# Two of the four weight sums of each Strassen unit made by transfers that add into SBUF

## The chip, the cores and the metric

The kernel runs on one core of one Trainium2 chip, as one program. The metric is device time in microseconds (us): the median of several runs. The engines are TensorE (PE in the profile, with its weight loads as PEld), VectorE (DVE), ScalarE (ACT), GpSimd (POOL) and SyncE (SP, which here only issues transfers). Each engine has one queue of its own that it works off in order; transfers are issued from an engine's queue and then carried out by the core's 16 DMA engines.

## The reference

The reference is one decoder layer on 512 tokens of width 1024 in float32: a half-step SwiGLU feed-forward network (FFN), a token mixer (a gated recurrence beside attention), and a second half-step FFN. The change touches only the last product of both FFNs, the one with `w_down`:

```
def _swiglu(x, w_gate, w_up, w_down):
    return (jax.nn.silu(x @ w_gate) * (x @ w_up)) @ w_down
...
x = x + 0.5 * _swiglu(_rms_norm(x, ffn1_norm[l]), ffn1_w_gate[l], ffn1_w_up[l], ffn1_w_down[l])
```

Here `w_gate` and `w_up` are 1024 x 2816, and `w_down` is 2816 x 1024.

## The kernel before

Everything is kept transposed: features lie on the 128 partitions, tokens along the free dimension. Float32 products are made from two parts each, a high part (a copy rounded to the format that PE multiplies fast, made by ACT at L127) and a low part (what is left, made by DVE at L129); a product is three matmuls, high by high, high by low and low by high. `parts` makes the two parts of a weight tile; `weights` loads a tile and calls it. The tiles of the high and low parts have four buffers each.

An FFN (`ffn`) treats the 2816 hidden features as 22 blocks of 128, in chunks of 6, 6, 6 and 4. `products(f)` makes the gate and up products of a block, and `hidden` scales them and combines them on DVE and ACT. For the first three chunks the down projection goes by Strassen's scheme in Winograd's form, which does a 2 x 2 block product with seven block products in place of eight. The blocks on the weights' side are pairs of hidden blocks against two output blocks of 128 (output block k and k + 4); on the other side are the two halves of 256 tokens. `operands` prepares the seven combinations of hidden blocks for a pair of hidden blocks.

One unit is `down(k, ...)`: output blocks k and k + 4 of one chunk, m = 3 pairs of hidden blocks, so w = 384 columns per weight block. It does four things:

- L319 and L320: SP loads the raw tile (tag "wd", two buffers), 128 x 4 x 384, 768 KB: the four weight blocks of the unit side by side.
- L321 to L327: DVE makes four sums of these blocks in the sums tile (tag "ws", two buffers): one instruction of 768 columns makes sums 1 and 2 (L323), and two of 384 columns make sum 0 (L326) and sum 3 (L327). The first of them is queued behind an instruction of `hidden` by `issue_after`.
- L329: the seven weight operands (raw blocks and sums) form four groups: raw 0 and 1; sums 0 and 1; sums 2 and 3; raw 3. `parts` makes the high and low parts of a group when its first product is traced (L337).
- L354 to L368: seven products (steps) of 9 matmuls, each followed by a DVE instruction at L350 that adds the partial result into `x`. Groups one to three serve two steps each, the fourth one step.

Units run in pairs, k = 0 and 1, then 2 and 3, and the loop at L381 interleaves the two units of a pair: two steps of the one, two of the other, and so on. There are 2 FFNs x 3 chunks x 4 units = 24 units, so 12 pairs; a stretch of down products (two pairs, 252 matmuls) stands between the `products` of one chunk and the next, six stretches in all. In the profile the tiles of the first FFN end in "a", those of the second in "b": `rda` and `rdb` are the raw tiles, `sda` and `sdb` the sums, `h_da` and `l_da` the high and low parts of a group, `pda` and `pdb` the PSUM results.

The last chunk of four blocks is done without the scheme (`down_plain`).

The program is written with a framework that draws the order of every engine's queue at build time, by simulating the whole program (`schedule_with_timeline_sim=True`, L951), subject to the program's data dependences, the buffers of each tag, and the explicit `issue_after` blocks. A changed instruction can therefore move others. Tiles that are opened later in the same SBUF space wait for the earlier ones to be released.

POOL works in three places: it adds up the squares for the norms (L167), takes the power for the reciprocal root (L186), and does parts of the mixer. It issues no transfer in the kernel before; all transfers are SP's.

On the host `_layout` brings the weights into the order in which they are loaded: `by_pairs` puts, for each chunk, the blocks of output block k and of k + 4 next to each other, and within each the even hidden blocks ahead of the odd ones.

Of the kernel before, what the change touches and what calls it, by code (L numbers as in the profile page):

```python
# [8 lines left out]
F32 = mybir.dt.float32  # L9
# [3 lines left out]
ALU = mybir.AluOpType  # L13
PSUM = bass.MemoryType.PSUM

P = 128
T = 512
D = 1024
KD = D // P
DFF = 2816  # L20
NF = DFF // P
# [28 lines left out]
def hybrid_layer_kernel(  # L50
# [17 lines left out]
    nc = tc.nc  # L68
# [18 lines left out]
    def f32(ap):  # L87
        return ap.bitcast(F32)

    def bank(name, tag="b"):  # L90
        return banks["pool"].tile([P, T], F32, tag=tag, name=name, bufs=banks["tags"][tag])
# [28 lines left out]
    def weights(src, name, n=KD * P, rows=1):  # L120
        raw = wpool.tile([P, n], F32, tag="wr", name=f"r_{name}")
        nc.sync.dma_start(raw if rows == 1 else raw.rearrange("p (k m) -> p k m", k=rows), src)
        return parts(raw, name, n)

    def parts(raw, name, n):
        hi = wpool.tile([P, n], F32R, tag="wh", name=f"h_{name}", bufs=4)
        nc.scalar.copy(hi, raw)  # L127
        lo = wpool.tile([P, n], F32R, tag="wl", name=f"l_{name}", bufs=4)
        nc.vector.tensor_sub(lo, raw, f32(hi))  # L129
        return hi, lo  # L130

    def weights_early(*args):
# [79 lines left out]
    def ffn(name, xn, wg, wu, wd, first, done):  # L212
# [20 lines left out]
        with tc.tile_pool(name=f"ffn_{name}", bufs=2, reuse_waits="tile") as fp:  # L233
# [81 lines left out]
            def down(k, col, m, bs, after):  # L315

                n = f"{name}{col}_{k}"
                w = m * P
                raw = fp.tile([P, 4, w], F32, tag="wd", name=f"rd{n}")  # L319
                nc.sync.dma_start(raw, wd[k, :, 4 * col * P : 4 * col * P + 4 * w])  # L320
                sums = fp.tile([P, 4, w], F32, tag="ws", name=f"sd{n}")  # L321
                with tc.issue_after(after.ins):
                    nc.vector.tensor_add(  # L323
                        sums[:, 1:3, :], raw[:, 2:3, :].to_broadcast([P, 2, w]), raw[:, 0:4:3, :][:, ::-1, :]
                    )
                nc.vector.tensor_add(sums[:, 0, :], raw[:, 0, :], sums[:, 1, :])  # L326
                nc.vector.tensor_add(sums[:, 3, :], raw[:, 1, :], sums[:, 0, :])  # L327
                flat = "p s w -> p (s w)"
                srcs = (raw[:, 0:2, :], sums[:, 0:2, :], sums[:, 2:4, :], raw[:, 3:4, :])  # L329
                ws = []  # L330
                banks_ = [bank(f"pd{n}_{c}", "y")[:, :TH] for c in range(2)]
                lo_, hi_ = x[k], x[k + KD // 2]

                def product(pt, group, half, b, start):
                    if group == len(ws):
                        src = srcs[group]
                        ws.append(parts(src.rearrange(flat), f"d{n}_{group}", src.shape[1] * w))  # L337
                    wh, wl = ws[group]
                    for i in range(m):
                        s = slice((half * m + i) * P, (half * m + i + 1) * P)  # L340
                        bh, bl = bs[i][0][:, b, :], bs[i][1][:, b, :]
                        for q, (p, a) in enumerate(((wh, bh), (wh, bl), (wl, bh))):
                            nc.tensor.matmul(  # L343
                                pt, p[:, s], a, start=start and i == 0 and q == 0,
                                stop=i == m - 1 and q == 2, skip_group_check=True,
                            )

                def collect(pt, xk, half, by):
                    t = slice(half * TH, (half + 1) * TH)
                    nc.vector.scalar_tensor_tensor(  # L350
                        xk[:, t], pt, by, xk[:, t], op0=ALU.mult, op1=ALU.add
                    )

                u, v = banks_  # L354
                steps = [
                    [(u, 0, 0, B11, True), (lo_, 0, 0.5)],
                    [(v, 0, 1, B21, True), (lo_, 0, 0.5)],
                    [(u, 1, 0, T2, False), (lo_, 1, 0.5)],
                    [(v, 1, 1, T1, True), (hi_, 1, -0.5)],
                    [(u, 2, 0, T3, False), (hi_, 1, -0.5)],  # L360
                    [(v, 2, 1, B22, False), (lo_, 1, 0.5)],
                    [(u, 3, 0, T4, False), (hi_, 0, -0.5)],
                ]
                for p, c in steps:
                    def step(p=p, c=c):
                        product(*p)
                        collect(p[0], *c)
                    yield step  # L368

            f0 = 0  # L370
            for nf in CHUNKS[:-1]:
                bs, after = [], None
                for i in range(nf // 2):
                    bs.append(operands(f0 + 2 * i, i))

                    after = hidden.last if i == nf // 2 - 2 else after
                f0 += nf
                ahead.append(products(f0))
                for k in range(0, KD // 2, 2):
                    two = [list(down(k + i, (f0 - nf) // 2, nf // 2, bs, after)) for i in range(2)]  # L380
                    for r in (slice(0, 2), slice(2, 4), slice(4, 6), slice(6, 7)):  # L381
                        for steps in two:
                            for step in steps[r]:
                                step()
# [332 lines left out]
    with tc.tile_pool(name="att", bufs=2, reuse_waits="tile") as ap:  # L717
# [108 lines left out]
        for j, pair in enumerate(pairs):  # L826
            ws = []
# [43 lines left out]
def _layout(x, ffn1_norm, ffn1_w_gate, ffn1_w_up, ffn1_w_down, mix_norm, w_in,  # L871
            conv_w, conv_b, rg_w_a, rg_b_a, rg_w_x, rg_b_x, rg_lambda,
            q_norm, k_norm, rnn_out_norm, attn_out_norm, w_out,
            ffn2_norm, ffn2_w_gate, ffn2_w_up, ffn2_w_down):
    import numpy as np

    def cols(v):
        return np.asarray(v).reshape(-1, P).T

    def by_block(w):  # L880

        k, n = w.shape
        return w.reshape(k // P, P, n // P, P).transpose(2, 1, 0, 3).reshape(n // P, P, k)

    def by_pairs(w):


        b = by_block(w).reshape(KD, P, NF, P)
        o, f0 = [], 0
        for nf in CHUNKS:  # L890
            order = [f0 + i for i in (*range(0, nf, 2), *range(1, nf, 2))]
            if f0 + nf == NF:
                order = range(f0, NF)
            half = [b[c : c + KD // 2][:, :, order].reshape(KD // 2, P, nf * P) for c in (0, KD // 2)]
            o += half
            f0 += nf
        return np.concatenate(o, axis=2)

    w = np.asarray(w_in)[0]
    qkv = w[:, 2 * DR :].reshape(KD // 2, 2, P, 3, DR).transpose(3, 0, 2, 1, 4)  # L900
    vecs = np.concatenate(
        [
            cols(ffn1_norm[0]), cols(mix_norm[0]), cols(ffn2_norm[0]), cols(conv_w[0]),
            cols(conv_b[0]), cols(rg_b_a[0]), cols(rg_b_x[0]), cols(rg_lambda[0]),
            cols(rnn_out_norm[0]), cols(attn_out_norm[0]),
            cols(np.tile(np.asarray(q_norm[0]), 2)), cols(np.tile(np.asarray(k_norm[0]), 2)),
        ],
        axis=1,
    )

    def blockdiag(b):
        b = np.asarray(b)[0]
        o = np.zeros((P, NJ, P), b.dtype)
        for n in range(2 * NJ):
            r = (n % 2) * HD
            o[r : r + HD, n // 2, r : r + HD] = b[n]
        return o.reshape(P, NJ * P)

    a = {
        "xT": np.asarray(x)[0].T.reshape(KD, P, T).transpose(1, 0, 2),  # L920
        "vecs": vecs,
        "w_rg": by_block(w[:, : 2 * DR]),
        "w_qkv": qkv.reshape(3, KD // 2, P, 2 * DR),
        "bd_a": blockdiag(rg_w_a),
        "bd_x": blockdiag(rg_w_x),
        "w_out": by_block(np.asarray(w_out)[0]),
        "wg1": by_block(np.asarray(ffn1_w_gate)[0]),
        "wu1": by_block(np.asarray(ffn1_w_up)[0]),
        "wd1": by_pairs(np.asarray(ffn1_w_down)[0]),
        "wg2": by_block(np.asarray(ffn2_w_gate)[0]),  # L930
        "wu2": by_block(np.asarray(ffn2_w_up)[0]),
        "wd2": by_pairs(np.asarray(ffn2_w_down)[0]),
    }
    return {n: np.ascontiguousarray(a[n]) for n in _INS}
# [21 lines left out]
```

## Time and profile before

| what | value |
|---|---|
| median of 3 runs | 944.1 us (943.86 to 945.71) |
| the profiled execution, its own time | 943.62 us |
| its span, first to last instruction | 941.8 us |
| mean granted clock of PE | 0.995 |
| busy: PE, DVE, ACT, POOL | 927.3, 670.6, 374.1, 110.9 us |
| transfers | 88.65 MB on one queue, 27.6% of 16 DMA engines' span |

A page's busy times are sums over the span; the span is what the profile sees, and the execution's own time is 1.8 us longer. A row of a group gives the line, engine, operation, output and inputs, shapes and count; then the total busy time in us, the mean of one in ns, and the idle time ahead with what ended it. A row of the timeline gives the start, the duration, the engine, the line and the operation, and in brackets how long the engine had been idle and what released it. A row of the waits gives who waited for whom, the total, the number of times and the longest. A row of the table by windows gives the stretch, its length, and for PE, PEld, DVE, ACT and POOL the busy time with the number of instructions, then PE's granted clock, the busy share of the DMA engines and the GB/s that they moved. Matmuls overlap, so that a row's duration is longer than the distance between two starts.

### The profile page before, as it was taken

Reading aid. Unit: us, or ns where it says so; the run is one execution under the profiler, and the core shown is the slowest. Engines: PE = TensorE matmul, PEld = TensorE weight load, DVE = VectorE, ACT = ScalarE, POOL = GpSimd, SP = SyncE. Lnnn points to the kernel's source line nnn. Section 1 sums busy time; section 2 is a strip of 40 time slices with the busy share of each in tenths; the row PEclk is TensorE's granted clock in tenths of the full one; section 3 lists DMA queues with packets and bytes.
Section 4 is the critical chain, followed back from the end, with each engine's and each line's share of the span. In section 5 each row is a group of like instructions: output and inputs, shape, how many; then the busy total and the mean of one; then the engine's idle time right before and its main releaser. Section 6 shows DMA issues by size and latency. Waiting matters only on the chain.

```text
span 941.8 us, 12498 instructions
## 1 busy us (share of the span) xinstructions
PE 927.3 (98%) x4906; PEld 785.5 (83%) x4906; DVE 670.6 (71%) x1001; ACT 374.1 (40%) x528; POOL 110.9 (12%) x79
## 2 busy tenths in 40 slices
PE   8999999999999999999999999999999999999998
PEld 6888988898889888888776567888988899889987
DVE  7696867686768649855768868387766777677753
ACT  7233433333333326446556744343333334333430
POOL 4000000000000004644431140500000000000000
PEclk9999999999999999999998999999999999999999
DMA  7530342035202423322110122421253125212312
GB/s 246 179 112 1 130 162 94 19 114 178 90 23 68 142 82 112 112 89 90 34 56 24 46 80 93 164 90 45 68 179 104 53 68 179 90 68 68 111 46 90
DMA packets 27066, 89.44 MB, mean 95 GB/s; under 512 B 3072, under 2 KB 5376, under 8 KB 27008
## 3 DMA queue, kind: packets, MB, share of 16 engines
q1 hardware_dynamic: 27008, 88.65, 27.6%
q8 instruction: 39, 0.64, 0.3%
q14 instruction: 19, 0.16, 0.0%
HBM read 86.54 MB, written 2.10 MB: 94 GB/s over the span
## 4 chain that ended last, share of the span: by engine, by line
PE 90%; DVE 4%; issue 2%; DMA 1%; ACT 1%; POOL 1%; SPq 1%; DVEq 0%; ACTq 0%; POOLq 0%
PE pda L343 10%; PE pdb L343 9%; PE pga L137 5%; PE pga L138 5%; PE pga L139 5%; PE pub L137 4%; PE pub L138 4%; PE pub L139 4%; PE pgb L137 4%; PE pgb L139 4%; PE pgb L138 4%; PE pua L138 4%; PE pua L137 4%; PE pua L139 4%; PE po L137 1%
## 5 line engine op out<-in xcount | busy, mean ns | idle before, releaser
L343 PE MATMUL pdb<-bhb,h_db 128*128 128x256 f32 x252 | 71.2, 284 | 0.0
L343 PE MATMUL pda<-bha,h_da 128*128 128x256 f32 x252 | 71.2, 284 | 0.0
L343 PE MATMUL pdb<-blb,h_db 128*128 128x256 f32 x252 | 71.0, 283 | 0.0
L343 PE MATMUL pda<-bla,h_da 128*128 128x256 f32 x252 | 71.0, 283 | 0.0
L343 PE MATMUL pdb<-bhb,l_db 128*128 128x256 f32 x252 | 70.5, 284 | 0.2 <-DVE l_db L129 0.2
L343 PE MATMUL pda<-bha,l_da 128*128 128x256 f32 x252 | 70.4, 283 | 0.0
L137 PE MATMUL pub<-xh_b,h_ub 128*128 128x512 f32 x176 | 68.7, 390 | 0.5 <-DVE yo L704 0.5
L137 PE MATMUL pgb<-xh_b,h_gb 128*128 128x512 f32 x176 | 68.7, 390 | 0.0
L139 PE MATMUL pgb<-xh_b,l_gb 128*128 128x512 f32 x176 | 68.5, 389 | 0.0
L139 PE MATMUL pub<-xh_b,l_ub 128*128 128x512 f32 x176 | 68.5, 389 | 0.0
L138 PE MATMUL pgb<-xl_b,h_gb 128*128 128x512 f32 x176 | 68.5, 389 | 0.0
L138 PE MATMUL pub<-xl_b,h_ub 128*128 128x512 f32 x176 | 68.5, 389 | 0.0
L137 PE MATMUL pga<-xh_a,h_ga 128*128 128x512 f32 x160 | 62.4, 390 | 0.0
L137 PE MATMUL pua<-xh_a,h_ua 128*128 128x512 f32 x160 | 62.3, 390 | 0.0
L139 PE MATMUL pga<-xh_a,l_ga 128*128 128x512 f32 x160 | 62.3, 389 | 0.0
L138 PE MATMUL pga<-xl_a,h_ga 128*128 128x512 f32 x160 | 62.3, 389 | 0.0
L139 PE MATMUL pua<-xh_a,l_ua 128*128 128x512 f32 x160 | 62.3, 389 | 0.0
L138 PE MATMUL pua<-xl_a,h_ua 128*128 128x512 f32 x160 | 62.2, 389 | 0.0
L167 POOL TENSOR_TENSOR sqa_m<-sqa_m,sq_m 128x512 f32<-128x512 f32 x7 | 11.8, 1679 | 325.4 <-issue 321.5
L246 DVE TENSOR_TENSOR uub<-pub,rb_b 128x512 f32<-128x512 f32 x22 | 15.2, 690 | 47.3 <-PE pub L139 47.3
L343 PEld LDWEIGHTS pda<-bha,h_da 128*128 128x128 f32 x252 | 48.3, 192 | 0.5
L343 PEld LDWEIGHTS pdb<-bhb,h_db 128*128 128x128 f32 x252 | 48.2, 191 | 0.5
(317 smaller groups left out, 2454.5 us busy)
## 6 DMA issues: line engine op xcount, KB each, us to landing
r_gb<-in_wg SPq DMA_DIRECT2D x22, 512.0 KB, 3.2
r_ub<-in_wu SPq DMA_DIRECT2D x22, 512.0 KB, 3.2
r_ga<-in_wg SPq DMA_DIRECT2D x20, 512.0 KB, 3.3
r_ua<-in_wu SPq DMA_DIRECT2D x20, 512.0 KB, 3.4
rda<-in_wd SPq DMA_DIRECT2D x12, 768.0 KB, 4.3
rdb<-in_wd SPq DMA_DIRECT2D x12, 768.0 KB, 4.5
x<-in_xT SPq DMA_DIRECT2D x8, 256.0 KB, 4.9
r_da<-in_wd SPq DMA_DIRECT2D x4, 512.0 KB, 3.5
```

Source lines behind the costliest of these rows:

```text
L137: nc.tensor.matmul(out_, wh, ah, start=start, stop=False)
L138: nc.tensor.matmul(out_, wh, al, start=False, stop=False)
L139: nc.tensor.matmul(out_, wl, ah, start=False, stop=stop)
L167: nc.gpsimd.tensor_add(self.acc, self.acc, sq)
L246: nc.vector.tensor_mul(u, pu, rb)
L343: nc.tensor.matmul(pt, p[:, s], a, start=start and i == 0 and q == 0, stop=i == m - 1 and q == 2, skip_group_check=True,)
```

## The change

The raw tile loses a block and the host puts the two output halves of a unit the other way round, so that block 0 of the four in memory is the one that goes into both of the first two sums. SP now copies block 0 twice into the sums tile, side by side (384 KB written). POOL issues a transfer that reads blocks 1 and 2 and adds them, in the DMA engines, to what lies there (384 KB). It has to wait until the copies have landed. SP loads blocks 1 to 3 as the raw tile (576 KB). What was raw block 0, 1, 2 and 3 is now block 2, 3, 0 and 1 in memory. Block 0, the old raw 2, is an operand of no group and is needed in the sums alone. DVE makes the other two sums with two instructions of 384 columns, the first of them queued by `issue_after` as L323 was. The four groups hold the same weights in the same order as before; two of them are now strided views, so `parts` takes a tile of three dimensions. The seven steps and all matmuls are as before.

```
--- before.py
+++ after.py
@@ -124,9 +124,12 @@
 
     def parts(raw, name, n):
         hi = wpool.tile([P, n], F32R, tag="wh", name=f"h_{name}", bufs=4)
-        nc.scalar.copy(hi, raw)
         lo = wpool.tile([P, n], F32R, tag="wl", name=f"l_{name}", bufs=4)
-        nc.vector.tensor_sub(lo, raw, f32(hi))
+        h, l = hi, lo
+        if len(raw.shape) == 3:
+            h, l = (t.rearrange("p (s w) -> p s w", s=raw.shape[1]) for t in (hi, lo))
+        nc.scalar.copy(h, raw)
+        nc.vector.tensor_sub(l, raw, f32(h))
         return hi, lo
 
     def weights_early(*args):
@@ -316,17 +319,17 @@
 
                 n = f"{name}{col}_{k}"
                 w = m * P
-                raw = fp.tile([P, 4, w], F32, tag="wd", name=f"rd{n}")
-                nc.sync.dma_start(raw, wd[k, :, 4 * col * P : 4 * col * P + 4 * w])
+                src = wd[k, :, 4 * col * P : 4 * col * P + 4 * w].rearrange("p (s w) -> p s w", s=4)
+
                 sums = fp.tile([P, 4, w], F32, tag="ws", name=f"sd{n}")
+                nc.sync.dma_start(sums[:, 0:2, :], src[:, 0:1, :].to_broadcast([P, 2, w]))
+                nc.gpsimd.dma_start(sums[:, 0:2, :], src[:, 1:3, :], accum_op=ALU.add)
+                raw = fp.tile([P, 3, w], F32, tag="wd", name=f"rd{n}")
+                nc.sync.dma_start(raw, src[:, 1:4, :])
                 with tc.issue_after(after.ins):
-                    nc.vector.tensor_add(
-                        sums[:, 1:3, :], raw[:, 2:3, :].to_broadcast([P, 2, w]), raw[:, 0:4:3, :][:, ::-1, :]
-                    )
-                nc.vector.tensor_add(sums[:, 0, :], raw[:, 0, :], sums[:, 1, :])
-                nc.vector.tensor_add(sums[:, 3, :], raw[:, 1, :], sums[:, 0, :])
-                flat = "p s w -> p (s w)"
-                srcs = (raw[:, 0:2, :], sums[:, 0:2, :], sums[:, 2:4, :], raw[:, 3:4, :])
+                    nc.vector.tensor_add(sums[:, 2, :], raw[:, 1, :], sums[:, 0, :])
+                nc.vector.tensor_add(sums[:, 3, :], raw[:, 2, :], sums[:, 2, :])
+                srcs = (raw[:, 1:3, :], sums[:, 0:4:2, :][:, ::-1, :], sums[:, 1:4:2, :], raw[:, 0:1, :])
                 ws = []
                 banks_ = [bank(f"pd{n}_{c}", "y")[:, :TH] for c in range(2)]
                 lo_, hi_ = x[k], x[k + KD // 2]
@@ -334,7 +337,7 @@
                 def product(pt, group, half, b, start):
                     if group == len(ws):
                         src = srcs[group]
-                        ws.append(parts(src.rearrange(flat), f"d{n}_{group}", src.shape[1] * w))
+                        ws.append(parts(src, f"d{n}_{group}", src.shape[1] * w))
                     wh, wl = ws[group]
                     for i in range(m):
                         s = slice((half * m + i) * P, (half * m + i + 1) * P)
@@ -891,7 +894,8 @@
             order = [f0 + i for i in (*range(0, nf, 2), *range(1, nf, 2))]
             if f0 + nf == NF:
                 order = range(f0, NF)
-            half = [b[c : c + KD // 2][:, :, order].reshape(KD // 2, P, nf * P) for c in (0, KD // 2)]
+            cols_ = (0, KD // 2) if f0 + nf == NF else (KD // 2, 0)
+            half = [b[c : c + KD // 2][:, :, order].reshape(KD // 2, P, nf * P) for c in cols_]
             o += half
             f0 += nf
         return np.concatenate(o, axis=2)
```

## The prediction

> **What bounds the kernel now.** I read the page first: its span, the busy times and the chain that ended last.
>
> ```profile
> span 941.8 us, 12498 instructions
> ...
> PE 927.3 (98%) x4906; PEld 785.5 (83%) x4906; DVE 670.6 (71%) x1001; ACT 374.1 (40%) x528; POOL 110.9 (12%) x79
> ...
> PE 90%; DVE 4%; issue 2%; DMA 1%; ACT 1%; POOL 1%; SPq 1%; DVEq 0%; ACTq 0%; POOLq 0%
> ```
>
> TensorE (PE) is busy for 927.3 of 941.8 us, and the change takes no matmul away. What is left to win is PE's idle 14.5 us, so the second view is who PE waited for, and the third the busy time of the engines in a stretch of down products (the last of six; the columns after the stretch's length are PE, PEld, DVE, ACT, POOL, then clock, DMA share, GB/s).
>
> ```profile
> PE pw L773 <- DVE be L765: 3.3, 3, 1.5
> PE pv L137 <- DVE natk L639: 2.4, 1, 2.4
> ...
> PE pdb L343 <- DVE l_db L129: 0.2, 1, 0.2
> ```
> ```profile
> 853.40:884.80 31.40, 31.22 (x257) 30.79 (x256) 27.56 (x52) 12.85 (x17) 0.00 (x0) 1.00 0.19 63
> ```
>
> The long waits are in attention and the value projection (L773, L137 for pv), which the change does not touch. In the down products (L343) PE waited once, for 0.2 us. VectorE (DVE) is 88% busy there (27.56 of 31.40), so it is close behind, and POOL does nothing. The order of work around that one wait comes from the timelines of DVE, ACT, SP and PE. Units 2 and 3 of the chunk (its second pair) are what is loaded late; "rdb" is the raw tile, "sdb" the sums.
>
> ```profile
> 856.92 0.95 DVE L129 TENSOR_TENSOR l_db<-sdb,h_db 128x768 fp32r<-128x768 f32 x1
> ...
> 858.60 0.96 DVE L129 TENSOR_TENSOR l_db<-sdb,h_db 128x768 fp32r<-128x768 f32 x1 [0.39 <-ACT h_db L127]
> ...
> 860.47 0.55 DVE L129 TENSOR_TENSOR l_db<-rdb,h_db 128x384 fp32r<-128x384 f32 x1
> ...
> 862.54 0.56 DVE L129 TENSOR_TENSOR l_db<-rdb,h_db 128x384 fp32r<-128x384 f32 x1
> ...
> 865.18 0.96 DVE L323 TENSOR_TENSOR sdb<-rdb 128x768 f32<-128x768 f32 x1 [0.48 <-DMA rdb<-in_wd]
> ...
> 866.39 0.95 DVE L129 TENSOR_TENSOR l_db<-rdb,h_db 128x768 fp32r<-128x768 f32 x1
> 867.26 0.55 DVE L326 TENSOR_TENSOR sdb<-rdb,sdb 128x384 f32<-128x384 f32 x1
> 867.73 0.42 DVE L350 SCALAR_TENSOR_TENSOR x<-pdb,x 128x256 f32<-128x256 f32 x1
> 868.45 0.96 DVE L323 TENSOR_TENSOR sdb<-rdb 128x768 f32<-128x768 f32 x1 [0.30 <-DMA rdb<-in_wd]
> ...
> 869.66 0.55 DVE L327 TENSOR_TENSOR sdb<-rdb,sdb 128x384 f32<-128x384 f32 x1
> 870.12 0.95 DVE L129 TENSOR_TENSOR l_db<-rdb,h_db 128x768 fp32r<-128x768 f32 x1
> ```
> ```profile
> 868.53 0.84 ACT L127 CAST h_db<-rdb 128x768 fp32r<-128x768 f32 x1 [2.43 <-DMA rdb<-in_wd]
> ```
> ```profile
> 861.04 2.41 SPq L320 DMA_DIRECT2D rdb<-in_wd  x2
> ```
> ```profile
> 870.67 0.28 PE L343 MATMUL pdb<-blb,h_db 128*128 128x256 f32 x1
> 871.13 0.39 PE L343 MATMUL pdb<-bhb,l_db 128*128 128x256 f32 x1 [0.18 <-DVE l_db L129]
> ```
> ```profile
> 853.45 8.65 PE pdb L343 x72
> ```
>
> Down matmuls follow each other every 8.65/72 = 0.12 us. The matmul at 871.13 should have started at 870.67 + 0.12 = 870.79: PE lost 0.34 us, because the low part of unit 3's first group ended at 870.12 + 0.95 = 871.07. It is the third matmul of its product, behind unit 2's 18, so the second pair began at 870.79 - 20 x 0.12 = 868.4. Reading back, DVE did two sums (L323, 868.45, and L327) ahead of that low part, and L323 waited for the raw tile. So this stretch is bound by PE, with a raw tile and a queue on DVE just in time behind it.
>
> **The change part by part.** Per unit, the 768-wide sum L323 goes and the two 384-wide ones stay:
>
> ```profile
> L323 DVE TENSOR_TENSOR sdb<-rdb 128x768 f32<-128x768 f32 x12 | 11.2, 955 | 1.7 <-DMA rdb<-in_wd 1.7
> ```
>
> Over 24 units that is 24 x 0.955 = 22.9 us of DVE's 670.6. On the path lies only what delays PE: the 0.34 us above, and smaller delays of the same kind in the five other stretches that no row lists as PE waits. The gain is between 0 and about 1; I take 0.4. The other 22.5 us lie beside PE work.
>
> Added: one SP transfer of 384 KB into the first two sums, one POOL transfer of 384 KB that adds two other blocks to them, and a raw tile of 576 KB in place of 768. The nearest rows give KB and median us from issue to landing:
>
> ```profile
> rdb<-in_wd SPq DMA_DIRECT2D x12, 768.0 KB, 4.5
> ...
> r_o<-in_w_out SPq DMA_DIRECT2D x8, 256.0 KB, 2.7
> r_o<-in_w_out SPq DMA_DIRECT2D x4, 512.0 KB, 3.2
> ```
>
> 384 KB lies at 3.0 us, 576 KB at 2.7 + 320 x 1.8/512 = 3.8. No row shows a transfer that adds, nor one issued by POOL. Bounds: below, a plain copy with SP's issue of 0.3, so 3.3 us; it could undercut that only if its bytes took no time. Above, its bytes are moved three times (source and destination fetched, the sum written), 2.7 + 896 x 1.8/512 = 5.9, with POOL's longest small instruction ahead of it (1.94, quoted below): 7.8. I take 3.0 + 1.9 = 4.9, as the plain copy is the nearest row. The Trainium skill (DMA: Bandwidth & Descriptors, section Bandwidth, and the fit in its anatomy of a GpSimd-issued transfer) has 2.0 us fixed plus bytes over 436 GB/s: 2.9 us as an estimate by that page, for a transfer that only copies; the sum would come out the same.
>
> Now the last stretch again. A sums tile is free when the low part of its pair's third group is made: 857.9 (856.92 + 0.95) and 859.6 for the two units; a raw tile with its fourth group, 861.0 and 863.1, as now. So SP issues the new sums at 857.9 and 859.6, landed at 860.9 and 862.6. POOL, which waits for the landing, has nothing else queued here (0.00 busy). The adds land at 860.9 + 4.9 = 865.8 and, with POOL free at 862.8, 867.7. The raw tiles land at 861.0 + 3.8 = 864.8, and at 863.1 + 3.8 + 0.8 = 867.7 (now the second one takes 5.3 and not 4.5, to 868.4, as the two overlap). Unit 2's first low part ends at 864.8 + 0.84 + 0.95 = 866.6; PE wants it at 868.6. DVE then does two sums (1.1) to 867.7 and, after ACT's copy (868.5), unit 3's low part and a collecting step (0.42): 869.9 against 870.8. So 0.34 goes, and next is PE itself.
>
> Behind the added wait: on POOL nothing; on DVE, which works in order, everything behind the sum that needs the added tile, above all unit 3's first low part. 870.8 - 0.95 - 0.42 - 1.1 = 868.3 is the latest landing that harms nothing: 7.4 us after the first transfer landed, 2.5 more than I take. For a chunk's first pair the loads run a products stage ahead. At the start of the second FFN POOL has other work:
>
> ```profile
> 589.70 11.22 POOL L167 TENSOR_TENSOR sqa_b<-sqa_b,sq_b 128x512 f32<-128x512 f32 x7 [21.78 <-issue]
> 607.22 1.94 POOL L186 TENSOR_TENSOR r_b<-m_b,mhalf 128x4 f32<-128x4 f32 x1 [6.30 <-DVE m_b L182]
> ```
> ```profile
> 586.90 0.86 SPq L320 DMA_DIRECT2D rdb<-in_wd  x2
> ```
> ```profile
> 606.16 0.79 PE pst_b L174 x8
> ```
>
> Its seven additions end at 600.9 and PE's row sums come at 606.2: 5.2 us cover a POOL that first waits for the new transfers (586.9 + 3.0 = 589.9) and issues two (3.9). I cost this at nothing; without cover, up to 4 us once.
>
> Sum: the profiled execution took 943.6 us (span 941.8, 1.8 around it). 943.6 - 0.4 = 943.2; the median of the runs is 944.1, 0.5 higher, giving 943.7. I forecast 943.5. About 0.2% (1.9 us) is what a measurement here can tell from no change.
>
> **The rivals.** *The add lands too late (slower).* The queue on DVE is the mechanism, unit 3's first low part the place, 7.4 us from landing to landing the point where it decides. My upper bound of 7.8 is past it, and nothing in the trace shows how fast the DMA engines add. At 9.5 us PE stands 2.1 us in each of six second pairs: 12.6. A stop of that length also costs clock:
>
> ```profile
> 470.00:472.70 2.70, 0.27 (x2) 0.00 (x0) 0.79 (x2) 0.63 (x1) 2.70 (x3) 0.96 0.02 5
> 472.70:476.00 3.30, 3.29 (x8) 2.61 (x9) 1.98 (x4) 1.27 (x2) 3.30 (x4) 0.51 0.00 0
> ```
>
> After 2.4 us of idle PE ran 3.3 us at clock 0.51, a loss of 1.6. Six of those at worst: 943.5 + 12.6 + 0 to 9.6 = 956 to 966; at 8 us, 947. Against it: the 2.5 us of room. Chance 0.22.
>
> *The DMA engines are the bound (slower).* Their share and rate, last two columns:
>
> ```profile
> 857.90:862.00 4.10, 4.10 (x36) 4.10 (x36) 3.15 (x7) 1.18 (x3) 0.00 (x0) 1.00 0.00 0
> ...
> 864.00:865.00 1.00, 1.00 (x10) 1.00 (x10) 0.42 (x1) 0.00 (x0) 0.00 (x0) 1.00 1.15 373
> ```
>
> They idle until 862.0, which covers the plain transfers of the sums, and are then full. From 862 on there would be two raw tiles (1.18 MB) and two adds (0.79 MB, or 1.57 if destinations are fetched too): 1.97 to 2.75 MB at some 350 GB/s is 5.6 to 7.9 us, so the last raw tile lands between 867.6 and 869.9; PE needs it by 870.8 - 0.95 - 0.84 = 869.0. Up to 0.9 us late, six times: 943.5 + 5.4 = 949. The Trainium skill says (DMA: Bandwidth & Descriptors, section Issuing engines are not separate DMA queues) that transfers issued by different engines share the same 16 DMA engines and interleave; by that rule POOL's queue adds no bandwidth, which speaks against the change. No run here shows two queues moving at once. Chance 0.11.
>
> *The planner's new order helps elsewhere (faster).* The order on each engine is drawn at build time for the whole program. Were the value projection's 2.4 us wait with its 1.6 us of slow clock gone, it would be 943.5 - 4.0 = 939.5. Nothing speaks for it but that orders can move. Chance 0.12, and 0.02 for the reverse.
>
> **How the numbers follow.** The forecast has 0.53: its own range is 941.7 to 945.4 (the gain of 0 to 1, the scatter of the runs, and 1.8 in case POOL's queue doubles what lies around the span). With the rivals: slower by over 0.2% 0.22 + 0.11 + 0.02 = 0.35 less 0.01 for lateness under 0.3 us, faster 0.12, same 0.54. The range reaches up to 956, where the late add's bad half (0.1) is left out, and down to 941, which leaves out most of the faster case (0.1).
>
> **What would show it.** Right: DVE busy about 648; L323 gone; PE busy 927 still and no wait of L343 above 0.2; POOL's adds landing within 7.4 us of the transfer ahead of them; L326 in second pairs not waiting for a DMA. Wrong: PE waits at L343 put down to DVE's low parts, DVE idle ahead of L326 with a DMA as releaser, a clock below 1.00 in the down stretches, or waits outside the FFNs that moved.

## The result, and the profile after

The changed kernel takes 968.13 us (median of 4 runs, 967.54 to 970.53) against 943.98 us (942.01 to 945.71) for the kernel before: a ratio of 1.0261, with a 95% interval of 1.0234 to 1.0288. It is 24 us slower, where 943.5 us was forecast.

The first view is the page: span, busy time of the engines, the DMA queues (packets, MB, share of the time of all 16 engines), and at the end the DMA issues (KB of each, median us from issue to landing).

```profile
span 965.9 us, 12599 instructions
PE 936.4 (97%) x4906; PEld 790.9 (82%) x4906; DVE 655.0 (68%) x977; ACT 374.4 (39%) x528; POOL 132.2 (14%) x103
...
q0 software_dynamic: 3456, 9.44, 5.5%
...
rda<-in_wd SPq DMA_DIRECT2D x12, 576.0 KB, 5.9
rdb<-in_wd SPq DMA_DIRECT2D x12, 576.0 KB, 7.3
sda<-in_wd SPq DMA_DIRECT2D x12, 384.0 KB, 3.5
...
sda<-in_wd POOLq DMA_DIRECT2D x12, 384.0 KB, 7.4
...
sdb<-in_wd POOLq DMA_DIRECT2D x12, 384.0 KB, 7.9
```

DVE has less to do, 655.0 us against 670.6, and the kernel is slower all the same. The raw tiles are a quarter smaller and land later: 5.9 and 7.3 us after their issue, where 768 KB took 4.3 and 4.5; of these two the prediction shows the second, and this is the first:

```profile
rda<-in_wd SPq DMA_DIRECT2D x12, 768.0 KB, 4.3
```

The adding transfers take 7.4 and 7.9 us. PE is busy for 9.1 us more (936.4 against 927.3) with the same 4906 matmuls, so some of them went slower, and it stands idle for 15 us more.

Who PE waited for (us in total, times, longest) says where:

```profile
PE pdb L346 <- ACT h_db L131: 4.2, 4, 1.6
PE pda L346 <- ACT h_da L131: 3.9, 5, 1.3
...
PE pdb L346 <- DVE l_db L132: 2.5, 3, 0.8
...
PE pda L346 <- DVE l_da L132: 2.2, 3, 0.8
PE pda L346 <- DVE x L353: 1.2, 1, 1.2
...
PE pdb L346 <- DVE x L353: 1.0, 2, 0.7
```

All the new waits are in the down products (L346, L343 before): 8.1 us for the high parts that ACT copies, 4.7 for DVE's low parts, 2.2 for the collecting step. That is 15.0, and with PE's 9.1 more busy time 24.1, the whole difference of the spans (965.9 less 941.8). From first to last matmul start, the six stretches of down products took 30.69, 30.78, 30.67, 30.84, 30.67 and 31.14 us before; they take 36.66, 35.32, 33.98, 34.12, 33.71 and 36.65 now, 25.65 more in all (some 1.6 came back elsewhere). These six lengths are the measure for every experiment below: their sum is 184.79 before and 210.44 after.

One stretch shows how it comes about, the third of the changed kernel, from 288.51 on. Its second pair of units is loaded like this on SP (issue; x2 means both units), and the adds on POOL:

```profile
293.12 2.07 SPq L325 DMA_DIRECT2D sda<-in_wd  x2
296.27 2.42 SPq L328 DMA_DIRECT2D rda<-in_wd  x2
```
```profile
296.83 0.86 POOL L326 DMA_DIRECT2D sda<-in_wd  x1 [76.20 <-DVE x L353]
298.83 0.86 POOL L326 DMA_DIRECT2D sda<-in_wd  x1 [1.14 <-PE pda L346]
```

So POOL was free, and an issue took it 0.86 us. What the engines did meanwhile (columns: window, its length, PE, PEld, DVE, ACT, POOL, then clock, DMA share and GB/s; a packet counts in the window in which it starts, so a share can pass 1):

```profile
293.00:296.80 3.80, 3.80 (x34) 3.80 (x34) 3.27 (x8) 1.31 (x2) 0.00 (x0) 1.00 0.59 138
296.80:299.00 2.20, 2.20 (x21) 2.20 (x20) 1.41 (x3) 0.51 (x1) 1.03 (x2) 1.00 0.85 235
299.00:301.00 2.00, 2.00 (x19) 2.00 (x19) 0.84 (x2) 0.00 (x0) 0.69 (x1) 1.00 0.85 177
301.00:303.00 2.00, 1.71 (x15) 1.50 (x13) 0.01 (x1) 0.83 (x1) 0.00 (x0) 1.00 1.06 235
303.00:305.00 2.00, 1.97 (x16) 1.97 (x17) 1.64 (x3) 0.00 (x0) 0.00 (x0) 1.00 1.06 315
305.00:307.00 2.00, 1.60 (x13) 1.38 (x12) 1.01 (x3) 0.09 (x1) 0.00 (x0) 1.00 0.62 129
```

The DMA engines are at or near full from 296.8 to 305, but at 177 to 315 GB/s, where the kernel before had 373 GB/s in a full window. So the engines spend time on more than the bytes that are counted. ACT, DVE and PE then stand in a row behind it:

```profile
306.91 0.83 ACT L131 CAST h_da<-rda 128x768 fp32r<-128x768 f32 x1 [3.93 <-DMA rda<-in_wd]
```
```profile
304.31 0.56 DVE L330 TENSOR_TENSOR sda<-rda,sda 128x384 f32<-128x384 f32 x1 [0.34 <-DMA sda<-in_wd]
...
307.32 0.56 DVE L330 TENSOR_TENSOR sda<-rda,sda 128x384 f32<-128x384 f32 x1 [1.31 <-DMA sda<-in_wd]
307.79 0.42 DVE L353 SCALAR_TENSOR_TENSOR x<-pda,x 128x256 f32<-128x256 f32 x1
308.13 0.55 DVE L331 TENSOR_TENSOR sda<-rda,sda 128x384 f32<-128x384 f32 x1
308.59 0.95 DVE L132 TENSOR_TENSOR l_da<-rda,h_da 128x768 fp32r<-128x768 f32 x1
```
```profile
307.79 0.39 PE L346 MATMUL pda<-bha,h_da 128*128 128x256 f32 x1 [1.20 <-ACT h_da L131]
308.02 0.28 PE L346 MATMUL pda<-bla,h_da 128*128 128x256 f32 x1
...
309.60 0.39 PE L346 MATMUL pda<-bha,l_da 128*128 128x256 f32 x1 [0.83 <-DVE l_da L132]
```

The raw tile of unit 3 lands at 306.9 (ACT starts on it then), 18.4 us after the stretch began; the prediction's latest harmless moment was 15.7 after it. PE stops for the high part (307.79). The adds land at 304.3 and 307.3, where the two sums L330 begin, the second after DVE stood in front of it for 1.31 us. Unit 3's low part could have begun when ACT was done (306.91 + 0.83 = 307.74); it began at 308.59, behind two sums and a collecting step, and PE stopped again (309.60). These two sums are unit 3's own: the first waits for the second add, and the second is made from it.

PE's busy time grew in two ways. The first is the clock. These rows are of the first stretch (the first two), the second and the sixth:

```profile
106.61:113.43 6.82, 6.28 (x29) 5.98 (x28) 6.01 (x10) 2.61 (x4) 0.00 (x0) 0.50 0.16 36
113.44:123.30 9.86, 9.86 (x83) 9.77 (x82) 6.83 (x14) 3.81 (x5) 1.72 (x2) 1.00 0.89 210
209.02:212.42 3.40, 3.19 (x15) 3.19 (x16) 3.40 (x7) 0.63 (x2) 0.00 (x0) 0.50 0.00 0
895.10:898.50 3.40, 3.40 (x18) 3.40 (x18) 3.35 (x7) 0.83 (x1) 0.00 (x0) 0.50 0.00 0
```

Among or just behind the stops of these three stretches the clock is halved for 6.8, 3.4 and 3.4 us, and then full again (second row); before, it is 1.00 in the down products. At half the clock 13.6 us hold at most 6.8 us of lost work. In the other three stretches the clock is not lowered, though PE waits there for 1.9 to 2.5 us each, against 2.4 to 3.4 in these. What decides this, no run shows. The second way is seen in the third stretch, here after and before:

```profile
288.51:322.49 33.98, 31.63 (x254) 30.73 (x253) 25.74 (x49) 11.99 (x16) 1.73 (x2) 1.00 0.36 88
```
```profile
278.61:309.28 30.67, 30.67 (x254) 30.51 (x253) 27.09 (x51) 12.69 (x17) 0.00 (x0) 1.00 0.18 60
```

At clock 1.00 PE is busy for 1.0 us more. Right behind the stop at 307.79 the next matmul starts 0.23 us later, where 0.12 is the rule in the down products; why is open. So there are PE's stops, a halved clock in three stretches, and some slow matmuls behind a stop.

### The profile page after: what moved, and what is told of

Same layout as the page of the kernel before. It is cut to its first block, busy times and chain, and to the rows that moved or that the text cites. A ratio compares the mean times of both kernels' runs of the same rounds, so it can differ in the third digit from the quotient of the medians.

```text
span 965.9 us, 12599 instructions
## 1 busy us (share of the span) xinstructions
PE 936.4 (97%) x4906; PEld 790.9 (82%) x4906; DVE 655.0 (68%) x977; ACT 374.4 (39%) x528; POOL 132.2 (14%) x103
## 3 DMA queue, kind: packets, MB, share of 16 engines
q0 software_dynamic: 3456, 9.44, 5.5%
## 4 chain that ended last, share of the span: by engine, by line
PE 57%; DVE 5%; DMA 4%; issue 2%; ACT 1%; POOL 1%; DVEq 0%; POOLq 0%; ACTq 0%
PE pdb L346 7%; PE pub L140 4%; PE pub L142 4%; PE pub L141 4%; PE pgb L140 4%; PE pgb L142 4%; PE pgb L141 4%; DMA sdb<-in_wd 3%; PE pga L142 1%; PE pga L140 1%; PE pda L346 1%; PE pga L141 1%; PE po L140 1%; PE po L141 1%; PE po L142 1%
## 5 line engine op out<-in xcount | busy, mean ns | idle before, releaser
L346 PE MATMUL pda<-bha,h_da 128*128 128x256 f32 x252 | 74.0, 294 | 5.1 <-ACT h_da L131 3.9
L346 PE MATMUL pdb<-bhb,h_db 128*128 128x256 f32 x252 | 73.1, 291 | 5.3 <-ACT h_db L131 4.2
L346 PE MATMUL pda<-bha,l_da 128*128 128x256 f32 x252 | 72.7, 292 | 2.2 <-DVE l_da L132 2.2
L346 PE MATMUL pdb<-bhb,l_db 128*128 128x256 f32 x252 | 71.3, 287 | 2.5 <-DVE l_db L132 2.5
L346 PE MATMUL pda<-bla,h_da 128*128 128x256 f32 x252 | 72.8, 290 | 0.0
L346 PE MATMUL pdb<-blb,h_db 128*128 128x256 f32 x252 | 71.8, 286 | 0.0
L346 PEld LDWEIGHTS pda<-bha,h_da 128*128 128x128 f32 x252 | 50.1, 199 | 6.9 <-ACT h_da L131 4.9
L346 PEld LDWEIGHTS pdb<-bhb,h_db 128*128 128x128 f32 x252 | 48.9, 194 | 7.7 <-ACT h_db L131 5.2
L346 PEld LDWEIGHTS pda<-bha,l_da 128*128 128x128 f32 x252 | 49.9, 200 | 2.9 <-DVE l_da L132 2.9
L346 PEld LDWEIGHTS pdb<-bhb,l_db 128*128 128x128 f32 x252 | 48.6, 194 | 3.1 <-DVE l_db L132 3.1
```

Source lines behind the costliest of these rows:

```text
L346: nc.tensor.matmul(pt, p[:, s], a, start=start and i == 0 and q == 0, stop=i == m - 1 and q == 2, skip_group_check=True,)
```

## The experiments

Two theories stood against each other. *Engines*: the new transfers take so much of the DMA engines' time in the few microseconds before the second pair that raw tiles and adds land late. *Queue*: the sum that waits for the add stands in DVE's order ahead of unit 3's low part, and holds it. Each kernel is compared with runs of the kernel before that were made beside it (943.49 us for the first four, 943.8 us for the last four).

**The sums behind the low parts.** DVE's two sums are ordered behind the low part of the second unit's first group, so a late add holds no low part of a first group.

```diff
-                with tc.issue_after(after.ins):
-                    nc.vector.tensor_add(sums[:, 2, :], raw[:, 1, :], sums[:, 0, :])
-                nc.vector.tensor_add(sums[:, 3, :], raw[:, 2, :], sums[:, 2, :])
...
+                        if group == 1:
+                            with tc.issue_after(down.low.ins):
+                                nc.vector.tensor_add(sums[:, 2, :], raw[:, 1, :], sums[:, 0, :])
+                            nc.vector.tensor_add(sums[:, 3, :], raw[:, 2, :], sums[:, 2, :])
```

> The change, with the two VectorE sums of a pair queued behind the low part of the second unit's first group. Theory 'queue' (a sum that waits for the late add holds VectorE's queue, and unit 3's low part with it): PE's waits for low parts (4.7 us) and for collecting steps (2.2 us) go, with about half of the 9 us that the lower clock costs: about 957 us. Theory 'engines' (the DMA engines are full while adds and raw tiles move, so the raw tiles themselves land late): unit 3's raw tile still lands some 8 us after its issue, PE's waits for high parts (8.1 us) stay, and the sums are now behind it: 964 to 970 us.

Measured: 971.74 us, ratio 1.0296 (1.0270 to 1.0321). It is no faster than the change. PE's waits for high parts are 11.1 us (8.1), for low parts 3.9 (4.7). The queue alone is not the cause. The six stretches take 3.3 us more than in the change, while the intervals of the two ratios overlap; why is open.

**A fourth raw tile.** Unit 2's and 3's raw tiles then load before the stretch, and only copies and adds remain in it.

```diff
-                raw = fp.tile([P, 3, w], F32, tag="wd", name=f"rd{n}")
+                raw = fp.tile([P, 3, w], F32, tag="wd", name=f"rd{n}", bufs=4)
```

> The change, with four buffers for the raw tiles (nothing else), so that the raw tiles of a chunk's second pair are loaded before the stretch of down products and not beside the adds. 'Engines': the waits for high parts go and most of what follows from them: 945 to 950 us. 'Queue': the adds still land 7 us or more after the copies and hold VectorE's queue: 956 to 963 us.

Measured: 971.69 us, ratio 1.0292 (1.0265 to 1.0318), which neither theory gave. The lengths explain why: 36.87, 36.28, 32.46, 36.36, 37.02, 34.44. With a tile to spare, the raw tiles of the next chunk load into the stretch, beside the adds. Only the last chunk of each FFN (third and sixth) has no next one; there the adds have the engines to themselves, and land 5.1 to 6.2 us after their issue. PE stops there too. Of the third stretch, first the engines' window during an add, then DVE:

```profile
298.70:301.80 3.10, 3.10 (x29) 3.10 (x28) 0.00 (x0) 1.37 (x2) 0.85 (x1) 1.00 0.98 154
```
```profile
301.82 0.56 DVE L330 TENSOR_TENSOR sda<-rda,sda 128x384 f32<-128x384 f32 x1 [3.26 <-DMA sda<-in_wd]
...
303.09 0.95 DVE L132 TENSOR_TENSOR l_da<-rda,h_da 128x768 fp32r<-128x768 f32 x1
```

Adds alone fill the engines (0.98) at 154 GB/s. And the raw tile had long been there, but DVE stood for 3.26 us in front of the sum, with the low part behind it. So the queue holds PE as well, once the raw tiles don't.

**Four sums tiles.** The copies and adds of the second pair run ahead of the stretch; a tile elsewhere changes its pool to make the room.

```diff
-                b = fp.tile([P, 2, TH], F32, tag="h", name=f"hf{n}")
+                b = fp.tile([P, 2, TH], F32, tag="b", name=f"hf{n}")
...
-                sums = fp.tile([P, 4, w], F32, tag="ws", name=f"sd{n}")
+                sums = fp.tile([P, 4, w], F32, tag="ws", name=f"sd{n}", bufs=4)
```

> The change, with four buffers for the sums tiles; for the space the hidden blocks of the last chunk take the buffers of the operands' scratch. The copies and adds of the second pair then land before the stretch begins. Both 'queue' and 'engines' say that all of the loss goes: 943 to 946 us. A third theory, a fixed cost of the change (strided views in the splitting, GpSimd's queue as such, another order elsewhere), says that most of it stays: 960 us or more.

Measured: 957.98 us, ratio 1.0144 (1.0112 to 1.0175), short of the 943 to 946 expected. The lengths are 34.37, 33.42, 30.56, 35.18, 33.63, 30.71: the last chunk of each FFN is back at its time of before, and in the four others the next chunk's copies and adds now run beside the second pair's raw tiles. The kernel's waits in the down products are for those raw tiles first:

```profile
PE pda L346 <- ACT h_da L131: 3.0, 3, 1.6
PE pdb L346 <- ACT h_db L131: 2.5, 4, 1.0
```

**A copy in place of the add.** POOL's transfer overwrites; the kernel leaves out the addition, and moves the same bytes.

```diff
-                nc.gpsimd.dma_start(sums[:, 0:2, :], src[:, 1:3, :], accum_op=ALU.add)
+                nc.gpsimd.dma_start(sums[:, 0:2, :], src[:, 1:3, :])
```

> The change, with GpSimd's transfer as a plain copy of the same bytes: it leaves out the addition, so that the first two sums hold copies of a block. It measures what adding costs beside copying. 'Queue': the transfer lands in under 6 us and not 7.5, which is within the room of 7.4, so that VectorE is not held: 944 to 949 us. 'Engines': the bytes are the same, the engines' time for the POOL queue falls from 2.2 us to about 1.2 us per transfer, so a part of the loss stays: 950 to 958 us. If the 24 us stay, neither adding nor its engine time is the cause.

Measured: 951.3 us, ratio 1.0085 (1.0061 to 1.0109). POOL's queue in its page:

```profile
q0 software_dynamic: 1920, 9.44, 2.8%
```

The same 9.44 MB take 1920 packets and 2.8% of a 949.6 us span, where the adds took 3456 and 5.5% of 965.9. For one of the 24 transfers that is 1.1 us of all 16 engines as a copy, 2.2 us as an add. The six lengths sum to 194.88: 10.1 us more than before, where the change has 25.65 more. Adding rather than copying makes 15.6 of the 25.65. The total lies where *engines* put it, not *queue*. But POOL's copies also land sooner (5.7 and 5.8 us after their issue), so this run does not part the two theories by itself.

**The kernel before, with the traffic.** The sums are made by DVE as before; the copy and the add go to two more rows of the sums tile, which nobody reads.

```diff
-                sums = fp.tile([P, 4, w], F32, tag="ws", name=f"sd{n}")
+                sums = fp.tile([P, 6, w], F32, tag="ws", name=f"sd{n}")
+                src = wd[k, :, 4 * col * P : 4 * col * P + 4 * w].rearrange("p (s w) -> p s w", s=4)
+                nc.sync.dma_start(sums[:, 4:6, :], src[:, 0:1, :].to_broadcast([P, 2, w]))
+                nc.gpsimd.dma_start(sums[:, 4:6, :], src[:, 1:3, :], accum_op=ALU.add)
```

> The kernel before, with the change's two transfers per unit (SP's copy of 384 KB and GpSimd's adding transfer of 384 KB) going beside its own 768 KB raw tile into two more rows of the sums tile that nothing reads; VectorE makes all four sums as before. 'Engines': the raw tiles land 6 to 9 us after their issue and not 4.5, and PE waits for high and low parts of second pairs: 955 to 966 us. 'Queue' alone: no instruction of VectorE waits for an adding transfer, so 944 to 946 us.

Measured: 961.14 us, ratio 1.0184 (1.0170 to 1.0197). These are its only waits in the down products, and its raw tiles:

```profile
PE pda L346 <- ACT h_da L127: 5.9, 6, 1.5
...
PE pdb L346 <- ACT h_db L127: 5.5, 6, 1.1
```
```profile
rda<-in_wd SPq DMA_DIRECT2D x12, 768.0 KB, 7.2
rdb<-in_wd SPq DMA_DIRECT2D x12, 768.0 KB, 6.6
```

No instruction waits for the added data, so DVE's queue plays no part, and still 17 us are lost: the raw tiles land 7.2 and 6.6 us after their issue (4.3 and 4.5 before). This shows the engines by themselves. The six lengths sum to 202.71, 17.9 more than before; though this kernel moves more than the change does, it loses 7.7 us less.

**Both: a fourth raw tile, and the sums behind the low parts** (the first two edits together).

> The change with both edits: four raw buffers, and the sums behind the low parts. In the last chunk of an FFN no next chunk's raw tiles are loaded beside the adds, and no low part waits behind a sum: if the loss there has just these two causes, those two stretches of down products take 30.7 to 31.3 us (34.0 and 36.7 in the change, 32.5 and 34.4 with four raw buffers alone). In the other four chunks the next chunk's raw tiles are loaded beside the adds and the adds land 7 to 9 us after their issue, which is now past the need of the second group: 33 to 37 us each. In all 955 to 966 us.

Measured: 955.43 us, ratio 1.0123 (1.0109 to 1.0136); lengths 33.79, 33.58, 30.68, 33.03, 33.38, 30.69. The last chunks' 32.46 and 34.44 of the second experiment, which differs only in the sums' place, have become 30.68 and 30.69. That is the queue, shown: 5.5 us in two stretches. What is left lies in the four others, and is a wait for neither part, but for the collecting step (DVE's x), which now stands behind the sums that wait for adds (L338). PE's waits, then DVE in the second stretch:

```profile
PE pda L349 <- DVE x L356: 4.3, 6, 1.6
PE pdb L349 <- DVE x L356: 3.3, 6, 1.2
```
```profile
204.70 0.56 DVE L338 TENSOR_TENSOR sda<-rda,sda 128x384 f32<-128x384 f32 x1 [2.66 <-DMA sda<-in_wd]
205.18 0.42 DVE L356 SCALAR_TENSOR_TENSOR x<-pda,x 128x256 f32<-128x256 f32 x1
```

Of the two edits, each alone gained nothing (213.75 and 213.43 us in the six stretches, 210.44 in the change); together they bring 195.15. Late raw tiles and late adds stand side by side: with either one mended, the other still holds PE.

**Four sums tiles, the next chunk's copies held.** As the third experiment, but SP's copies for a chunk are issued only behind the last raw tile of the chunk before, so that nothing new shares the engines with a second pair's raw tiles.

```diff
-                nc.sync.dma_start(sums[:, 0:2, :], src[:, 0:1, :].to_broadcast([P, 2, w]))
+                with tc.issue_after(down.held.ins) if down.held else nullcontext():
+                    nc.sync.dma_start(sums[:, 0:2, :], src[:, 0:1, :].to_broadcast([P, 2, w]))
...
-                nc.sync.dma_start(raw, src[:, 1:4, :])
+                down.raw = nc.sync.dma_start(raw, src[:, 1:4, :])
```

> The change with four buffers for the sums tiles and the copies of the next chunk queued on SP behind the raw tiles of this one, so that neither copies nor adds run while the second pair's raw tiles are loaded. 'Engines': the raw tiles land about 4 us after their issue, all six stretches take 30.6 to 31.0 us, in all 942.5 to 945 us, the time of the kernel before. If a stretch still takes over 32 us, something other than transfers in that window is at work.

Measured: 945.43 us, ratio 1.0010 (0.9991 to 1.0029): the time of the kernel before, if a little above the range expected. Its page, and a window of its first stretch:

```profile
PE 930.0 (98%) x4906; PEld 787.4 (83%) x4906; DVE 653.9 (69%) x977; ACT 375.2 (40%) x528; POOL 131.2 (14%) x103
...
q0 software_dynamic: 3456, 9.44, 5.9%
...
rda<-in_wd SPq DMA_DIRECT2D x12, 576.0 KB, 4.9
```
```profile
104.00:118.00 14.00, 13.85 (x110) 13.29 (x110) 11.57 (x23) 5.33 (x7) 1.85 (x3) 1.00 0.93 214
```

The same transfers run, the adds no cheaper (5.9% of 945.9), and the engines are full for most of those 14 us (0.93); but nothing on the path waits for them any more. The lengths are 31.21, 30.56, 31.17, 31.24, 31.46 and 30.72, 186.36 in all. So it is when the added engine time falls that costs, not that it exists. This kernel clears the engines and the wait in DVE's queue at once and cannot part them; that the engines cost by themselves is shown by the fifth experiment, that the queue does by the sixth. And it answers the other half of the question: with the loss gone, DVE's 16.7 us less busy time (653.9 against 670.6) bring nothing that can be measured. Its 12 runs scatter more (940.35 to 950.87) than those of the kernel before (942.19 to 946.16); why is open.

**One sum by transfer.** Half the change: 192 KB copied, 192 KB added, raw tiles of 768 KB, three sums on DVE.

```diff
-                nc.sync.dma_start(sums[:, 0:2, :], src[:, 0:1, :].to_broadcast([P, 2, w]))
-                nc.gpsimd.dma_start(sums[:, 0:2, :], src[:, 1:3, :], accum_op=ALU.add)
+                nc.sync.dma_start(sums[:, 0, :], src[:, 0, :])
+                nc.gpsimd.dma_start(sums[:, 0, :], src[:, 1, :], accum_op=ALU.add)
```

> Half the dose: one of the four sums by transfer (a copy of 192 KB, an adding transfer of 192 KB), the raw tile of 768 KB, three sums of 384 columns on VectorE. By the shares of the queues the DMA engines need 2.3 us per unit before, 5.3 with the change and about 4.0 here. 'Engines': the loss is between a third and a half of the change's: 950 to 956 us. If the number of adding transfers and not their size set the loss: 964 us or more.

Measured: 958.48 us, ratio 1.0158 (1.0142 to 1.0174), above what was expected. In the six stretches (32.99, 32.03, 32.23, 31.99, 31.89, 33.18) it loses 9.5 us, 37% of the change's 25.65, so the loss does shrink with the added bytes. POOL's queue:

```profile
q0 software_dynamic: 3456, 4.72, 2.9%
```

Half the bytes take as many packets as in the change and about half the share of the engines, so here the engines' time goes by the bytes added and not by the packets. The rest of the loss came from elsewhere: the order drawn for the whole program moved, and PE waits once for 3.9 us ahead of the first stretch, for a DVE step (gga, L245) that it does not wait for in the change. That is the side effect that the prediction gave 0.02.

## Why the prediction was wrong

*DVE's gain.* Right for the path, not for DVE's busy time. The L323 groups are gone (22.4 us), and the time they took was not on the path: with the transfers held out of the way the kernel takes what it took before. DVE's busy time fell by 15.6, not 22.9; one known part of the difference is 1.6 us in the FFN's low parts, the rest is open.

*The copy of 384 KB.* Nearly right: 3.5 us against 3.0.

*The landing of the add.* This is the term that failed first. It was put at 4.9 us after the copy's landing, with an upper bound of 7.8 that charged each byte three times at the rate of a plain load. Issue to landing took 7.4 and 7.9 us in the median; in the stretch shown, with the wait for POOL, the two adds landed 8.0 and 9.0 us after the copies (from 296.3 and 298.3 to 304.3 and 307.3). Even with the engines to themselves they took 5.1 to 6.2 us from issue. Two things were missing: an add takes twice the engine time of a copy (2.2 against 1.1 us), and it shares the engines with the raw tiles.

*The landing of the raw tiles.* This is the step that cost the most. It gave each tile 3.8 us, as if it moved alone, with 0.8 for the second. With the engines free that is about right: where the third experiment has no adds beside them, in the last chunks, the tiles land 3.6 to 4.3 us after their issue. In the stretch shown they take 5.8 and 8.5 us, since two raw tiles and two adds want the engines at once. So unit 3's tile came 18.4 us into the stretch and not 14.4; 15.7 was the limit, and past it PE did stop. The traffic alone, without any new wait, cost 17 us in the fifth experiment.

*The rival of the DMA engines.* It had the mechanism and the place, with a chance of 0.11, and 949 us where 968 was measured. Its bytes were about right: two adds at 1.57 MB and 350 GB/s are 4.5 us, two measured adds 4.4 us. Mis-sized were two other terms. It ended the transfers with their bytes: 7.9 us from 862.0 on, that is from 1.0 us after the issue of the raw tiles, where a 256 KB load takes 2.7 us for 0.7 us of bytes, 2.0 us more. With the missing 1.0 the tile would have come at 870.9, which is 17.6 us into the stretch (from 853.3), against 18.4. And it charged the lateness alone (0.9 us, six times): measured were 2.7 us of lateness in the stretch shown, waits of 2.5 us a stretch in the mean (15.0 over six), and 9.1 us of added busy time of PE on top. The rival had no term for a lower clock, to which at most 6.8 us of slower work in the stretches goes, although the queue's rival had one. The Trainium skill (DMA: Bandwidth & Descriptors, section Issuing engines are not separate DMA queues) says that queues of different engines share the 16 DMA engines; the trace agrees, with full engines at 177 to 315 GB/s and raw tiles that land 1.6 and 2.8 us later in the median than the larger ones of before.

*The rival of the late add.* Right in its mechanism and its threshold (7.4 us between the landings; 8.0 and 9.0 came), and its 956 to 966 us lie close to 968. That nearness is in part luck: 8.1 of PE's 15.0 us of waits are for ACT's high parts, which this rival did not have. As the cause it is only a part: the sums behind the low parts gained nothing by themselves. Low parts and collecting steps make 6.9 of PE's 15.0 us of waits, and the change loses 7.7 us more in its stretches than the kernel before with the traffic and no reader. One step of the order was also missed: the prediction put only unit 2's two sums ahead of unit 3's low part. In the trace unit 3's own two stand there too, and so the second add, which lands 18.8 us into the stretch and was put at 14.4, holds that low part.

*The start of the second FFN.* Costed at nothing, and right: PE has no wait for the row sums (pst_b). In the last-but-one experiment, where the loads run further ahead and POOL's adds lie between its additions, one of 1.2 us appears.

*The path of the error.* Each transfer was priced by a row in which it had the engines nearly to itself, and the sum of the engines' time over the window, which would have shown that they can't all land, was made for the rival only. From the raw tiles' issue (296.3) to unit 3's limit (288.5 + 15.7 = 304.2) lie 7.9 us; two raw tiles at 350 GB/s take 3.4 us of all engines and two adds 4.4, so 7.8 us, with nothing left for the time to start and to land. Of the signs of being wrong that were named, PE's waits for low parts, DVE idle ahead of the sum (L330, L326 before) and a clock below 1.00 came; the largest group of waits, for ACT's high parts, was not among them.

## What to carry to other kernels

Before a transfer takes over an engine's work, add up the DMA engines' time in the window before its data is needed, all queues together, and put the fixed time of issue and landing on top; a mean share (5.5% for the adding queue here) says nothing about a window that is full. Time saved on an engine that PE did not wait for bought nothing here, and a new wait on that engine still held all that stood behind it in its order. Where two late arrivals stand side by side, mend both in one experiment before dropping either as a cause.

## What the hardware showed that was not expected

- A transfer that adds into SBUF takes 2.2 us of all 16 DMA engines for 384 KB, against 1.1 us as a plain copy from the same queue, with 3456 packets in place of 1920. For 192 KB, in as many packets, it is about half (2.9% of the span against 5.5%). Alone it fills the engines (0.98) at 154 GB/s.
- PE's stops in the changed kernel are at most 1.6 us long. In three stretches the granted clock was 0.50 among or just behind them, for 6.8, 3.4 and 3.4 us; in the three others, with waits of much the same length, it stayed at 1.00.
